# Pools that begin at multiples of 128 bytes, and feed-forward matmuls whose moving operand is read from its last column to its first

## The chip, the cores and the metric

The kernel runs on one core of one Trainium2 chip. The metric is device time in microseconds of one execution: the median of 3 runs before the change is 2208.15 us (2207.96 to 2208.68). Less is better. TensorE (PE in the profile) does the matmuls; PEld is its weight load; VectorE is DVE, ScalarE is ACT, GpSimd is POOL, and SP issues DMAs.

## The reference, cut to what matters

One layer of an encoder over 1024 tokens of width 1024, all in float32: a half-weighted SwiGLU feed-forward, a mixer of two attention branches, and a second feed-forward.

```python
def swiglu(h, w1, w3, w2):
    return (jax.nn.silu(h @ w1) * (h @ w3)) @ w2
...
    h = modulate(x, norm_g[l, 0], mod[:, 0, 0], mod[:, 0, 1])
    x = x + 0.5 * mod[:, 0, 2][:, None, :] * swiglu(h, ffn1_w1[l], ffn1_w3[l], ffn1_w2[l])
    h = modulate(x, norm_g[l, 1], mod[:, 1, 0], mod[:, 1, 1])
    y = hybrid_mixer(h, w_in[l], fox_f_bias[l], ...)
    x = x + mod[:, 1, 2][:, None, :] * y
    h = modulate(x, norm_g[l, 2], mod[:, 2, 0], mod[:, 2, 1])
    x = x + 0.5 * mod[:, 2, 2][:, None, :] * swiglu(h, ffn2_w1[l], ffn2_w3[l], ffn2_w2[l])
```

The hidden width of a feed-forward is 2816. The mixer projects `h`, runs attention over 8 heads with a decay (fox) and over 8 heads with the 256 best keys of an index score (dsa), gates both and projects back.

## The kernel before, in words

Activations lie transposed: 128 features on the partitions, tokens along the free dimension, in halves of 512 tokens. A float32 product is made of three fp32r matmuls (`mm3`, line 465): every operand is split into a high and a low part, and high times high, high times low and low times high are added up in one PSUM bank. So a matmul has a *stationary* operand (128 columns of weights, loaded by a LDWEIGHTS of its own) and a *moving* operand (512 columns that stream through the array).

**The feed-forwards.** Each is done by Strassen's scheme with 7 block products in place of 8. The first half (`UpPair`, line 1496; called up below) runs over 11 pairs of 128 hidden features. A pair has 14 products (7 for each of the two weight matrices), a product runs over 4 blocks of 128 input features, and each block is one `mm3`: 11 x 14 x 4 x 3 = 1848 matmuls with 512 moving columns. Their moving operands are the blocks of `h` in `k.B`: `b11`, `b21`, `b22`, `t1` to `t4`. The gated result is stored in HBM (`d_g`). The second half (`Down`, line 1660) has 7 products over 11 blocks and 4 outputs: 7 x 11 x 4 x 3 = 924 matmuls, again with 512 moving columns, which are blocks of `d_g` read back and split. Up and down of both feed-forwards are 3696 and 1848 matmuls, 5544 together.

**Where operands lie.** SBUF is handed out by pools that begin where the one before them ends. The pool of constants, which is the first on the left, ends 64 bytes past a multiple of 128 in the built program. Tiles are multiples of 128 bytes nearly everywhere, so a pool's tiles all have its remainder. On the right side the pools grow down from an end that is 96 bytes past a multiple of 128. In the built program:

| moving operand of | home | bytes past a multiple of 128 | its weights | matmuls |
|---|---|---|---|---|
| up 1: `b11`, `b21` | `h0`, right | 96 | 96 | 528 |
| up 1: the other five | `h1`, `common0`, left | 64 | 96 | 1320 |
| up 2: `b11`, `b21`, `t2`, `t3` | `h0b`, `h1`, left | 64 | 96 | 1056 |
| up 2: `t1`, `t4`, `b22` | `common`, right | 32 | 96 | 792 |
| down 1 and 2 | same pool as the weights | 96 | 96 | 1848 |

The 528 matmuls of the branches' first part and of the output projection that take `h` tiles have 64 against 96 too.

**The order of the work** is made by a planner (`Plan`, line 213). Every call is recorded as a task with the tiles that it reads and writes; `flush` places the tasks engine by engine by modelled costs, and the program is written in that order. What a task depends on is found from `View.region` (line 136): the part of a tile that a view touches. It looks at the *first* indexing of a view alone; a second indexing of the same view does not narrow the region. Waits on the chip come from the real addresses, not from these regions.

**The attention.** `att_scores` (line 1150) makes the scores of a pair of heads. `mn` is a small tile of 8 columns: the row minima of up to four score tiles go into columns 0 to 3 (by a DVE reduction that also adds the bias, a `CUSTOM_DVE_ANT_0` in the profile and an `ISA pr,mn` in the program), and the sums of the exponentials into columns 4 to 7 (by ACT).

Of the kernel before, what the change touches and what calls it, by code (L numbers as in the profile page):

```python
# [9 lines left out]
F32 = mybir.dt.float32  # L10
# [87 lines left out]
class View:  # L98
# [37 lines left out]
    def region(self):  # L136

        if not self.ops or self.ops[0][0] != "__getitem__":
            return ()
        i = self.ops[0][1][0]  # L140
        r = []
        for j, n in zip(i if isinstance(i, tuple) else (i,), self.tile.full):
            if isinstance(j, slice):
                a, b, step = j.indices(n)
                r.append((a, b))
            elif isinstance(j, int):
                r.append((j, j + 1))
            else:
                break
        return tuple(r)  # L150
# [314 lines left out]
def mm3(k, out, w_hi, w_lo, m_hi, m_lo, start, stop, onto=False):  # L465

    mm = k.nc.tensor.matmul
    kw = dict(skip_group_check=True) if onto else {}
    mm(out, w_hi, m_hi, start=start and not onto, stop=False, **kw)
    mm(out, w_hi, m_lo, start=False, stop=False, **kw)  # L470
    mm(out, w_lo, m_hi, start=False, stop=stop, **kw)
# [82 lines left out]
class Ring:  # L554
# [7 lines left out]
    def raw(self):  # L562
        p, n = self.raws[self.j % len(self.raws)]
        self.j += 1
        return p.tile([128, D], F32, tag="wr", name="wr", bufs=n)
# [23 lines left out]
def t512(k, dt=F32, name="t", home="c"):  # L589

    p, tag, n = k.homes[home]
    return p.tile([128, H], dt, tag=tag, name=name, bufs=n)


class Halves:
# [13 lines left out]
    def raw(self, src, i, home="c", name="wr"):  # L609

        t = t512(self.k, name=name, home=home)
        self.k.nc.sync.dma_start(t, src[:, i * H:i * H + H])
        return t


def part8(w, c):
# [34 lines left out]
def chunks(w):  # L651

    return (1, w) if w <= 512 else (2, w // 2)
# [7 lines left out]
def pview(t, w):  # L661
    n, m = chunks(w)
    return t[:, :w].rearrange("p (a b) -> p a b", a=n)
# [486 lines left out]
def att_scores(k, p, two, j, ps2):  # L1150

    nc = k.nc
    pr = [[], []]
    mn = p.tile([128, 8], F32, tag="mn", name="mn", bufs=6)
    for qbs in ([(2 * j, 2 * j + 1)] if j < 2 else [(2 * j,), (2 * j + 1,)]):
        ps = [ps2() for _ in range(2)]
        nc.want(*ps)
        at = {}
        nc.group = 1 - nc.group
        for qb in qbs:  # L1160
            n, m = chunks((qb + 1) * 128)
            at[qb] = [(qb % 2 if j < 2 else i) * 512 for i in range(n)]
            for i, o in enumerate(at[qb]):
                last = two.diag and i == n - 1
                for t, (a, b) in enumerate(((0, 0), (1, 0), (0, 1))):
                    for h in range(2):
                        r = slice(64 * h, 64 * h + 64)
                        nc.tensor.matmul(ps[h][:, o:o + m], two.q[a][r, qb * 128:qb * 128 + 128],
                                         two.kk[b][r, i * m:i * m + m], start=t == 0, stop=t == 2 and not last)
        for qb in qbs if two.diag else ():  # L1170
            o = at[qb][-1] + chunks((qb + 1) * 128)[1]
            for h in range(2):
                nc.tensor.matmul(ps[h][:, o - 128:o], k.ident_b, k.causal_b, start=False, stop=True)
        nc.group = -nc.group
        yield
        for qb in qbs:
            w = (qb + 1) * 128
            n, m = chunks(w)
            for h in range(2):
                c = 2 * (qb % 2) + h  # L1180
                t = p.tile([128, T], F32, tag="pr", name="pr", bufs=8)
                s = ps[h].rearrange("p (a b) -> p a b", a=2)[:, at[qb][0] // 512:at[qb][0] // 512 + n, :m]
                nc.vector.tensor_tensor_reduce(pview(t, w), s, pview(two.addend(h, qb), w), op0=ALU.add, op1=ALU.min,
                                               scale=1.0, scalar=3e38, accum_out=mn[:, c:c + 1])
                nc.scalar.activation(t[:, :w], t[:, :w], AF.Exp, scale=-1.0, bias=mn[:, c:c + 1],
                                     accum_out=mn[:, 4 + c:5 + c])
                pr[h].append(t)
            yield
    nc.vector.reciprocal(mn[:, 4:8], mn[:, 4:8])
    for h in range(2):  # L1190
        for i, t in enumerate(pr[h]):
            w, c = (2 * j + i + 1) * 128, 4 + 2 * i + h
            nc.gpsimd.tensor_scalar(t[:, :w], t[:, :w], mn[:, c:c + 1], 1.0, op0=ALU.mult, op1=ALU.mult)
        yield
    two.pr = pr
# [219 lines left out]
PAIRS = NF // 2  # L1415


class Operands:
# [26 lines left out]
    def block(self, c):  # L1445

        self.scale(c, 0)
        self.pair("b11" if c < 4 else "b21", self.x[c][0], self.shift(c), "h0")
# [47 lines left out]
class UpPair:  # L1496
# [36 lines left out]

    def block(self, ps, w, b, c, onto=False):
        s = slice(c * 128, c * 128 + 128)
        mm3(self.k, ps, w[0][:, s], w[1][:, s], *self.k.B[b][c], c == 0, c == 3, onto)

    def product(self, src, b, onto=None, bank=None):

# [120 lines left out]
class Down:  # L1660
# [85 lines left out]
    def run(self, steps={}):  # L1746

        k = self.k
        for p, (first, _, early) in enumerate(self.ORDER):
            if p != 1:  # L1750
                ps = [(k.seeded if p in (2, 4, 6) else self.bank)() for _ in range(4)]
            if p == 2:
                for d in range(4):
                    k.nc.scalar.activation(ps[d], self.u[d], AF.Copy)
            ops = []

            def mms(d, q):
                w, m = ops[q]
                c = slice(d * 128, d * 128 + 128)
                mm3(k, ps[d], w[0][:, c], w[1][:, c], *m, q == 0, q == PAIRS - 1, p in (1, 2))  # L1760

            together = PAIRS - 3 if p == 6 else PAIRS
            for q in range(PAIRS):
                for f in steps.get((p, q), ()):
                    f()
                self.step += 1
                self.stores()
                self.loads(p * PAIRS + q + 1 + self.LEAD)
                if early == "s2":
                    self.sum("s2", q)  # L1770
                w = self.wq.split(self.a[first][q])
                ops.append((w, self.wq.split(self.g.pop((p, q)))))
                if early not in (None, "s2"):
                    self.sum(early, q)
                if q < together:
                    for d in range(4):
                        mms(d, q)
            for d in range(4):
                for q in range(together, PAIRS):
                    mms(d, q)  # L1780
                self.out(p, d, ps[d])
                if p == 6 and self.s == 2:
                    self.stores(True)
# [175 lines left out]
def layer(tc, xT, c, pos, ada_w, ada_b, ng, inv, w13a, w2a, w_a, w_f, w_q, w_g, fb, fg, dg, wbr, wout, w13b, w2b, out):  # L1959
    with ExitStack() as es:  # L1960
        k = K()
        k.nc = nc = Plan(tc)

        def pool(stack, name, own=False, **kw):
            if kw.get("space") != DRAM:
                kw["reuse_waits"] = "tile"
            return LatePool(nc, stack.enter_context(tc.tile_pool(name=name, bufs=1, **kw)), kw.get("space"), own)

        k.c = pool(es, "const")
        hp = [None, pool(es, "h1", True)]  # L1970
        k.h_tile = lambda hf, dt=F32R: hp[hf].tile([128, H], dt, tag="h", name="h", bufs=16)
        dp = pool(es, "dram", space=DRAM)
# [48 lines left out]
        with ExitStack() as ph:  # L2021
            k.wq = wq = Halves(k, pool(w0s, "w0", True, side="right"), 8, [nc.vector, nc.gpsimd])
            rp = k.c
# [197 lines left out]
            ps = [k.seeded() for _ in range(4)]  # L2221
# [18 lines left out]
        sp = pool(s3, "s")  # L2240
        k.s = {qb: sp.tile([128, (qb + 1) * 128], F32, name=f"s{qb}") for qb in range(2, 8)}
        k.mask = {qb: sp.tile([128, (qb + 1) * 128], BF16, name=f"mk{qb}") for qb in range(2)}
        for qb in range(2):
            nc.gpsimd.memset(k.mask[qb], 0.0)
            nc.gpsimd.memset(k.mask[qb][0:64, qb * 128 + 64:qb * 128 + 128], BIG)
        k.thr = sp.tile([128, 6], F32, name="thr")
        fox = ExitStack()
        fp = pool(fox, "fox", True, side="right")
        nc.on, nc.window = True, 600
# [22 lines left out]
        ps = ExitStack()  # L2272
# [19 lines left out]
        with ExitStack() as ph:  # L2292
# [9 lines left out]
            for i in range(2):  # L2302
                a, b = (ap.tile([128, H], F32R, tag=f"pz{j}", name=f"pz{j}", bufs=2) for j in "hl")
# [28 lines left out]
        with ExitStack() as ph:  # L2332
            hp[0] = pool(ph, "h0b", True)
            k.wq = wq = Halves(k, pool(ph, "w3", True, side="right"), 8, [nc.vector])
            rp = pool(ph, "rms", True, side="right")
            k.homes = {"h0": (hp[0], "h", 16), "h1": (hp[1], "h", 16), "g": (Pairs(nc, w2, (("wr", 2), ("wh", 2), ("wl", 2))), "g", 12),
                       "c": (pool(ph, "common", True, side="right"), "t", 41)}
            m = br.rest(lambda: next(both))
# [120 lines left out]
```

## Time and profile before

| what | before |
|---|---|
| median of 3 runs | 2208.15 us |
| the profiled execution's span | 2205.4 us |
| its PE busy | 2159.9 us (98%) |
| its DVE busy | 1639.2 us (74%) |
| its ACT busy | 1133.7 us (51%) |
| its POOL busy | 222.1 us (10%) |

The profile tells one execution. Its page gives each engine's busy time; the chain of waits follows back from the last instruction what released what, and merges neighbouring matmuls of one tile name into a row (start in us, length in us, what, count), so a row's length over its count is the time from one matmul's start to the next one's. A table by windows gives each engine's busy time in a stretch. Matmuls overlap in their pipeline, so a matmul's own duration (about 390 ns for 512 columns) is longer than its distance to the next.

By time: the first feed-forward is at 0 to 690 us (down from 466), projections and index scores at 690 to 1025, attention at 1025 to 1380, branches and output at 1380 to 1490, the second feed-forward's up at 1490 to 1991 and its down to the end.

### The profile page before, as it was taken

To read this page: it belongs to the slowest core of one execution; us is meant where nothing else is said; L and a number is where in the kernel's file an instruction comes from. 1 tells how busy PE (TensorE), PEld (TensorE's weight loads), DVE (VectorE), ACT (ScalarE), POOL (GpSimd) and SP (SyncE) were. 2 spreads that over 40 slices of the span, in tenths; PEclk is the share of its full clock that TensorE was granted. 3 is DMA by queue.
4 is the path that set the end of the run, shared out by engine and by line. 5 is a ranking of instruction groups with operands and counts; after the bars stand their busy time and mean duration, and the time that the engine had idled before them with its cause. 6 is when DMAs were issued, how large, how long until landed. Compare 5 with 4: busy or idle time off the path is not lost.

```text
span 2205.4 us, 31519 instructions
## 1 busy us (share of the span) xinstructions
PE 2159.9 (98%) x10700; PEld 1777.8 (81%) x10700; DVE 1639.2 (74%) x3095; ACT 1133.7 (51%) x2101; POOL 222.1 (10%) x229
## 2 busy tenths in 40 slices
PE   7999999999999999999999999999999999999999
PEld 5877888877888999987787777778778888888887
DVE  7977887689876498886896677598865756558665
ACT  4744444445455476776766677234443333334443
POOL 0000212100010201001343233000000000000000
PEclk9999999999999999999999999999999999999999
DMA  9245887699521325456343313696123542367521
GB/s 331 101 134 183 265 281 253 237 360 335 158 88 52 116 91 187 143 162 227 104 155 113 113 48 96 235 340 187 46 76 134 163 124 87 106 215 276 170 74 39
DMA packets 208734, 364.15 MB, mean 165 GB/s; under 512 B 29734, under 2 KB 57382, under 8 KB 208572
## 3 DMA queue, kind: packets, MB, share of 16 engines
q1 hardware_dynamic: 208572, 362.13, 49.1%
q8 instruction: 84, 1.38, 0.3%
q14 instruction: 78, 0.64, 0.1%
HBM read 265.85 MB, written 96.20 MB: 164 GB/s over the span
## 4 chain that ended last, share of the span: by engine, by line
PE 86%; DVE 6%; ACT 3%; DMA 2%; issue 2%; SPq 0%; POOL 0%; DVEq 0%; ACTq 0%; POOLq 0%
PE bs L433 34%; PE b L433 28%; PE pj L433 7%; PE py L433 7%; PE p L433 7%; PE pt L433 3%; DVE xc L433 1%; DVE macc L433 1%; ACT pr L433 1%; DVE wl L433 1%; ACT pth L433 1%; DVE xb L433 1%; DVE ptl L433 0%; SPq L433 0%; DMA gw<-in_w_f 0%
## 5 line engine op out<-in xcount | busy, mean ns | idle before, releaser
L433 PE MATMUL bs<-h,wh 128*128 128x512 f32 x1728 | 542.0, 395 | 1.4 <-ACT bs L433 1.3
L433 ACT ACTIVATE wh<-wr 128x512 fp32r<-128x512 f32 (+1 forms) x330 | 207.3, 638 | 359.0 <-PE bs L433 166.9
L433 PEld LDWEIGHTS bs<-h,wh 128*128 128x128 f32 x1728 | 323.2, 188 | 80.8 <-ACT bs L433 4.8
L433 PE MATMUL b<-h,wh 128*128 128x512 f32 x1088 | 345.2, 397 | 5.2 <-ACT z L433 2.6
L433 PE MATMUL bs<-h,wl 128*128 128x512 f32 x864 | 338.8, 394 | 1.0 <-DVE wl L433 1.0
L433 DVE TENSOR_TENSOR wl<-wr,wh 128x512 fp32r<-128x512 f32 x308 | 209.8, 704 | 127.1 <-ACT wh L433 120.6
L433 PEld LDWEIGHTS b<-h,wh 128*128 128x128 f32 x1088 | 204.9, 189 | 56.1 <-ACT z L433 3.5
L433 PE MATMUL b<-h,wl 128*128 128x512 f32 x544 | 214.9, 395 | 0.7 <-DVE wl L433 0.7
L433 PEld LDWEIGHTS bs<-h,wl 128*128 128x128 f32 x864 | 162.2, 188 | 40.2 <-DVE wl L433 1.9
L433 ACT ACTIVATE wh<-a 128x512 fp32r<-128x512 f32 x132 | 83.3, 631 | 168.6 <-PE b L433 97.5
L433 DVE TENSOR_TENSOR wl<-a,wh 128x512 fp32r<-128x512 f32 x132 | 91.5, 693 | 84.5 <-ACT wh L433 80.6
L433 PE MATMUL b<-wh 128*128 128x512 f32 x352 | 137.2, 390 | 0.7 <-ACT mrow L433 0.7
L433 PE MATMUL b<-wl,wh 128*128 128x512 f32 x352 | 137.0, 389 | 0.0
L433 PE MATMUL b<-wh,wl 128*128 128x512 f32 x352 | 137.0, 389 | 0.0
L433 PEld LDWEIGHTS b<-h,wl 128*128 128x128 f32 x544 | 103.0, 189 | 25.6 <-DVE wl L433 1.6
L433 POOL TENSOR_SCALAR pr<-pr,mn 128x128 f32<-128x128 f32 (+7 forms) x128 | 100.3, 803 | 162.3 <-DVE mn L433 122.5
L433 DVE TENSOR_TENSOR z<-bs,z 128x512 f32<-128x512 f32 x116 | 79.4, 687 | 48.2 <-PE bs L433 27.7
L433 DVE TENSOR_TENSOR wl<-g,wh 128x512 fp32r<-128x512 f32 x154 | 107.0, 695 | 4.2 <-ACT wh L433 4.2
L433 PE MATMUL bs<-wl,wh 128*128 128x512 f32 x264 | 102.8, 391 | 2.1 <-DVE wl L433 1.9
L433 ACT ACTIVATE pr<-pr,mn 128x256 f32<-128x256 f32 (+7 forms) x128 | 98.3, 770 | 11.9 <-DVE mn L433 11.6
L433 DVE SCALAR_TENSOR_TENSOR macc<-mraw,cond,macc 128x512 f32<-128x512 f32 x119 | 96.5, 811 | 10.4 <-DMA mraw<-in_ada_w 8.6
L433 PE MATMUL pj<-wh,h 128*128 128x384 f32 x384 | 102.8, 338 | 0.0
(324 smaller groups left out, 4430.9 us busy)
## 6 DMA issues: line engine op xcount, KB each, us to landing
d_g<-z SPq DMA_DIRECT2D x154, 256.0 KB, 2.0
g<-d_g SPq DMA_DIRECT2D x154, 256.0 KB, 4.4
mraw<-in_ada_w SPq DMA_DIRECT2D x144, 256.0 KB, 5.3
wr<-in_w13a SPq DMA_DIRECT2D x112, 256.0 KB, 5.1
wr<-in_w13b SPq DMA_DIRECT2D x88, 256.0 KB, 4.9
a<-in_w2a SPq DMA_DIRECT2D x44, 256.0 KB, 5.3
a<-in_w2b SPq DMA_DIRECT2D x44, 256.0 KB, 5.4
gw<-in_w_g SPq DMA_DIRECT2D x32, 256.0 KB, 5.2
```

The source lines that it names most:

```text
L433: getattr(getattr(self.tc.nc, e), t.op)(*map(real, t.a), **{n: real(v) for n, v in t.kw.items()})
```

## The change

It has two parts and a helper.

1. Padding. A tile of 64 bytes in front of the constants, one of 96 bytes at the right end of SBUF (a pool of its own, `edge`), one of 96 bytes behind `thr` and one of 64 bytes in the pool `rms`. The tile `mn` is made 32 columns wide, of which the first 8 are used. In the built program every moving and stationary tile of the table above then begins at a multiple of 128 bytes.
2. Direction. `back(t)` is the view `t[:, ::-1]`. All 5544 feed-forward matmuls read their moving operand through it. An up product therefore comes out with its 512 tokens in reverse, is stored so, and down reads it in reverse again, which restores the order. Weights are read as before.
3. `View.region` gives the right bounds for a step of minus one.

```diff
-                r.append((a, b))
+                r.append((a, b) if step > 0 else (b + 1, a + 1))
...
+def back(t):
+
+    return t[:, ::-1]
...
-    mn = p.tile([128, 8], F32, tag="mn", name="mn", bufs=6)
+    mn = p.tile([128, 32], F32, tag="mn", name="mn", bufs=6)[:, 0:8]
...
-        mm3(self.k, ps, w[0][:, s], w[1][:, s], *self.k.B[b][c], c == 0, c == 3, onto)
+        mm3(self.k, ps, w[0][:, s], w[1][:, s], *map(back, self.k.B[b][c]), c == 0, c == 3, onto)
...
-                mm3(k, ps[d], w[0][:, c], w[1][:, c], *m, q == 0, q == PAIRS - 1, p in (1, 2))
+                mm3(k, ps[d], w[0][:, c], w[1][:, c], *map(back, m), q == 0, q == PAIRS - 1, p in (1, 2))
...
         k.c = pool(es, "const")
+        k.c.tile([128, 16], F32, name="pad0")
+        pool(es, "edge", side="right").tile([128, 24], F32, name="pad1")
...
         k.thr = sp.tile([128, 6], F32, name="thr")
+        sp.tile([128, 24], F32, name="pad2")
...
             rp = pool(ph, "rms", True, side="right")
+            rp.p.tile([128, 16], F32, name="pad3")
```

Up to the start of attention every engine's instructions stand in the same order as before; tiles' numbers differ. In attention they move, because of `mn`: it is now a view whose first indexing is `[:, 0:8]`, so its columns all have the same region, and the planner takes every write to one of its columns to wait for each earlier use of any other. On DVE, at the first score blocks of attention (`p_10515` holds the scores of the first head, `p_10517` of the second), stood before:

```order
L433 ISA pr,mn<-p_10515,f 128x128
L433 ISA mn 128x1
L433 ISA pr,mn<-p_10515,f 128x256
L433 ISA mn 128x1
L433 TENSOR_SCALAR tke,tkn<-s_7159,thr 128x384
L433 ISA pr,mn<-p_10517,f 128x128
L433 ISA mn 128x1
L433 ISA pr,mn<-p_10517,f 128x256
```

and now, with `p_10521` the first head's scores and `p_10523` the second's:

```order
L433 ISA pr,mn<-p_10521,f 128x128
L433 ISA mn 128x1
L433 TENSOR_SCALAR tke,tkn<-s_7164,thr 128x384
L433 ISA pr,mn<-p_10523,f 128x128
L433 ISA mn 128x1
L433 TENSOR_SCALAR tkn<-tkn 128x1
L433 TENSOR_SCALAR tke<-s_7164,thr 128x384
L433 ISA pr,mn<-p_10521,f 128x256
```

The reductions of one pair of heads now have other DVE work (the masks' `tke`, `tkn`) between them, and the second block of 256 columns comes after both heads' first. On ACT, at the same place, the exponentials (`pr,mn<-pr,mn`) and the evacuations of other matmuls (`gt`, `qs`, `pzh`, `yt`) stood before:

```order
L433 ACTIVATE pr,mn<-pr,mn 128x128
L433 ACTIVATE pr,mn<-pr,mn 128x256
L433 ACTIVATE pr,mn<-pr,mn 128x128
L433 ACTIVATE pr,mn<-pr,mn 128x256
L433 ACTIVATE gt<-py 128x512
L433 ACTIVATE pzh<-pt 128x384
L433 ACTIVATE pr,mn<-pr,mn 128x384 x2
```

and now:

```order
L433 ACTIVATE pr,mn<-pr,mn 128x128 x2
L433 ACTIVATE gt<-py 128x512
L433 ACTIVATE pr,mn<-pr,mn 128x256
L433 ACTIVATE qs<-pt,g_645 128x512 x2
L433 ACTIVATE pr,mn<-pr,mn 128x256
L433 ACTIVATE pr,mn<-pr,mn 128x384
L433 ACTIVATE pzh<-pt 128x384 x2
```

The exponentials are spread out, with the evacuations between them. From here to the first matmuls of the second feed-forward, orders differ on all engines; behind that they are the same again.

## The prediction

> **What bounds the kernel now.** The page first: how full is each engine, and what is the chain that ended last made of?
>
> ```profile
> span 2205.4 us, 31519 instructions
> PE 2159.9 (98%) x10700; PEld 1777.8 (81%) x10700; DVE 1639.2 (74%) x3095; ACT 1133.7 (51%) x2101; POOL 222.1 (10%) x229
> PEclk9999999999999999999999999999999999999999
> PE 86%; DVE 6%; ACT 3%; DMA 2%; issue 2%; SPq 0%; POOL 0%; DVEq 0%; ACTq 0%; POOLq 0%
> ```
>
> PE is busy nearly throughout, the chain is PE's for 86% of the span, and the clock is granted in every slice. So time is won by making matmuls follow each other faster, and hardly otherwise. Then the table by windows, one for each stage (the two ups, the two downs, attention):
>
> ```profile
> 68.00:466.00 398.00, 395.91 (x1702) 316.91 (x1701) 318.24 (x488) 184.84 (x329) 55.22 (x41) 1.00 0.65 218
> 466.00:690.00 224.00, 221.78 (x985) 181.14 (x984) 184.97 (x303) 118.36 (x208) 11.99 (x9) 1.00 0.57 194
> 1025.00:1380.00 355.00, 342.70 (x2371) 274.40 (x2370) 268.62 (x603) 240.98 (x540) 119.04 (x143) 1.00 0.37 118
> 1490.00:1991.00 501.00, 497.72 (x2153) 401.18 (x2152) 332.74 (x543) 199.43 (x340) 0.00 (x0) 1.00 0.40 129
> 1991.00:2205.40 214.40, 209.74 (x924) 172.97 (x923) 142.53 (x223) 90.55 (x159) 0.00 (x0) 1.00 0.40 132
> ```
>
> The columns are the window, its length, and busy time of PE, PEld, DVE, ACT and POOL, the clock and the DMA share. In the feed-forwards (rows 1, 2, 4, 5) PE lacks 2 to 5 us per stage, and DVE comes next with 318 of 398, 185 of 224, 333 of 501 and 143 of 214 us: 80, 83, 66 and 66%.
>
> Last the chain in order of time, in whose rows neighbouring matmuls are merged. It gives the pace, which is what the change is about:
>
> ```profile
> 68.72 32.33 PE bs L433 x142
> 281.21 11.21 PE bs L433 x48
> 1706.75 10.99 PE bs L433 x48
> 1717.73 11.20 PE b L433 x48
> 1990.97 59.85 PE b L433 x264
> ```
>
> All five rows are matmuls with 512 moving columns at the full clock, and they have four paces. Row 1 is up 1 on `b11`: 32.33 / 142 = 227.7 ns. Row 2 is up 1 on the later operands: 11.21 / 48 = 233.5 ns. Row 3 is up 2 on operands from `common`: 10.99 / 48 = 229.0 ns. Row 4 is up 2 on `h0b` and `h1`: 233.3 ns. Row 5 is down 2: 59.85 / 264 = 226.7 ns. Beside the table of places this sorts itself: with moving operand and weights at the same remainder of 128 bytes (96 and 96) the pace is 226.7 to 227.7 ns; 64 bytes apart it is 229.0; 32 bytes apart, 233.4. So here the place of an operand sets the pace, by up to 6.7 ns a matmul.
>
> **Part 1, the padding.** It makes every relation zero. In the ups 1320 + 1056 = 2376 matmuls go from 233.4 to 226.7 ns, 2376 x 6.7 = 15.9 us; 792 go from 229.0 to 226.7, 1.8 us; 528 and the downs' 1848 have the relation already. Outside the feed-forwards the 528 matmuls of branches and output run at the worst pace too:
>
> ```profile
> 1397.56 2.80 PE bs L433 x12
> ```
>
> 2.80 / 12 = 233.3 ns, so 528 x 6.6 = 3.5 us more. Other projections may gain a little; I count nothing. Sum of the padding: 21.2 us. All of it lies on PE, which sets the end there. The pads themselves are never read or written.
>
> **Part 2, the direction.** The trace has no matmul that reads backwards, so I bound it from both sides. What could a matmul lose at most? A row with 384 columns gives the part that does not grow with them:
>
> ```profile
> 823.05 4.16 PE pj L433 x24
> ```
>
> 4.16 / 24 = 173.3 ns for 384 columns against 226.7 for 512: 0.417 ns a column, so 213.5 ns of a 512-column matmul are streaming and 13.2 ns are fixed. If the direction took all of that away, 5544 x 13.2 = 73 us would go. In the other direction the nearest row is the worst relation, 233.4 ns: if a backward read stood as badly as that everywhere, the feed-forwards would be 528 x 5.7 + 792 x 4.4 + 1848 x 6.7 = 18.9 us slower than before. Farther off stands a matmul at half the clock:
>
> ```profile
> 28.40:31.50 3.10, 3.10 (x8) 2.46 (x8) 3.10 (x6) 2.71 (x6) 0.00 (x0) 0.50 1.05 387
> 28.97 0.63 PE L433 MATMUL b<-h,wl 128*128 128x512 f32 x1
> 29.40 1.05 PE L433 MATMUL b<-h,wh 128*128 128x512 f32 x2
> ```
>
> There one follows the other after 0.43 us at a granted clock of 0.50 (the column before the DMA share). A stream at half the rate would add 5544 x 0.2 = 1109 us.
>
> I take a gain of 6.7 ns, about half the fixed part: the rows show one step of 6.7 ns between the worst and the best relation of two reads, and I take one further step of that size. The reason: the pace hangs on how moving operand and weights lie to each other, so some of the fixed part is their reads' getting in each other's way; and in the built program each weight load is encoded from its last column to its first. Today the two reads run towards each other, afterwards both run downwards from the same remainder. That this helps is an inference; 0 and 13.2 ns stay as ends. 5544 x 6.7 = 37.1 us.
>
> [...]
>
> **Part 3, the moved instructions of attention.** No wait is added on the chip, but DVE's reductions and ACT's exponentials stand in another order.
>
> ```profile
> L433 PE MATMUL p<-qs 64*128 64x512 f32 (+5 forms) x576 | 67.7, 358 | 3.0 <-DVE mn L433 2.7 <-DVE qs L433 0.3
> L433 ACT ACTIVATE pr<-pr,mn 128x256 f32<-128x256 f32 (+7 forms) x128 | 98.3, 770 | 11.9 <-DVE mn L433 11.6
> ```
>
> PE's next scores wait for the reductions to free their bank, today for 2.7 us in all. The cover is PE's other work (projections of the gates, values), queued in order. At worst the second head's reduction of each of 8 pairs and 8 row blocks comes later by one exponential, 64 x 0.77 = 49 us; at best the 355 - 342.7 = 12.3 us that PE idles in attention go. The value is nearest to the small wait: I take +4 us.
>
> **The sum.** 21.2 + 37.1 = 58.3 us off PE. Not all arrives: DVE at 80 to 83% of the first feed-forward goes to some 85% (318 of 398 - 20 us in the up), and waits for DMAs stay as long as they are. I pass on nine tenths, 52.5 us. With attention's 4 us: 48.5 us, so a span of 2156.9 us. The median of the runs is 2.75 us above the profiled span (2208.15 against 2205.4), which makes 2159.7, said as 2160 us.
>
> **The rivals.**
>
> *The direction is indifferent.* Then only the padding is left: 21.2 x 0.9 - 4 = 15 us, 2193 us. For it: the trace has no case of a backward read, and Part 1 stands without it. Against it: reads that disturb each other by their places should also do so by their directions. [...]
>
> *The direction takes the whole fixed part.* 21.2 + 73 = 94 us, of which I pass on 0.85, since DVE in the first feed-forward would then be 87 to 88% busy; less 4 us: 2132 us. [...]
>
> *Slower: the backward read stands badly.* It starts at the last column, 4 bytes below a multiple of 128, and moves against the addresses. If the pace is then that of the worst relation, 233.4 ns everywhere, ups and downs lose 18.9 us, output and branches win 3.5, attention costs 4: 2208.15 + 19.4 = 2228 us. It decides once the feed-forwards' mean passes the present one, (2376 x 233.4 + 792 x 229.0 + 528 x 227.7 + 1848 x 226.7) / 5544 = 230.0 ns. For it: the downs have the best pace already, so 1848 matmuls have that to lose. Against: row 5's pace shows that a relation of zero is good at least forwards. The half-rate read belongs here too, as a far end.
>
> *Nothing happens on PE.* If the paces came from the stages' other work and not from places, only attention's 4 us would remain: 2212 us. Rows 3 and 4 speak against it: they are neighbours in the same stage with the same work, and differ by 4.3 ns.
>
> **How the numbers follow.** Forecast (both parts gain): 0.45. Indifferent: 0.28. Whole fixed part: 0.08. Worst relation or half rate: 0.14. Nothing: 0.05. A measurement of this kernel can tell some 0.2%, 4.4 us, from no change. Faster are the first three, 0.81; within 0.2% is the last, 0.05 (2212 is 0.17% up); slower 0.14. The range reaches from the whole fixed part, 2130, to 2212: it takes in the forecast, the indifferent case, most of the gain's upper end and the case of nothing, and leaves out the slower ones and what lies under 2130, under 0.2. Attention's own ends (-12 to +49 us) are in it only with the forecast and the indifferent case.
>
> **What would show it.** In the chain of the changed kernel 48 up matmuls take 220.0 x 48 = 10.56 us under the forecast, 10.88 if the direction is indifferent, 10.25 if the fixed part goes, 11.2 under the worst relation; a down row of 264 takes 58.1, 59.8, 56.4 or 61.6 us. All up rows should have one pace, whatever the tile: if 11.2 and 10.99 us still stand side by side, the reading of the places is wrong. Output rows of 12 should take 2.72 us. In attention's window PE's idle time should be 12 to 20 us; more means that the moved reductions cost. If the rows show the paces but the span does not follow, DVE or DMAs end the chain in the first feed-forward.

## The result and the profile after

| kernel | median | against before |
|---|---|---|
| before | 2208.06 us (2207.57 to 2208.68) | |
| changed | 2227.57 us (2226.55 to 2230.98) | ratio 1.0097, 95% interval 1.0085 to 1.0108 |

The change makes the kernel 19.5 us slower. The forecast was 2160 us and its range ended at 2212; what happened is the rival "the backward read stands badly", for which the prediction had 2228 us and a chance of 0.14.

The page of the changed kernel first: span, busy time of the engines, and the shares of the chain that ended last.

```profile
span 2229.3 us, 31511 instructions
PE 2173.5 (97%) x10700; PEld 1776.1 (80%) x10700; DVE 1639.2 (74%) x3095; ACT 1133.6 (51%) x2101; POOL 221.4 (10%) x229
PEclk9999999999999999999999999999999999999999
PE 84%; DVE 6%; DMA 4%; ACT 3%; issue 2%; SPq 0%; POOL 0%; DVEq 0%; ACTq 0%; POOLq 0%
```

The same number of matmuls, the same granted clock (mean 0.998 before, 0.997 here), DVE's and ACT's busy time unchanged (1639.2 and 1133.7 us before): PE is still the bound. It lies busy for 13.6 us more and idle for 10.3 us more (2229.3 - 2173.5 = 55.8, before 45.5). So the loss has two sources, one in the matmuls' pace and one in waits. (The profiled execution took 2230.98 us, 3.4 us above the median; so these differences add up to 23.9 us and not to 19.5.) The chain in order of time (start, length, what, count) shows the pace:

```profile
70.68 33.15 PE bs L433 x142
...
273.09 11.20 PE b L433 x48
284.29 11.20 PE bs L433 x48
...
1705.64 11.20 PE bs L433 x48
...
1733.64 11.20 PE b L433 x48
...
2009.04 61.60 PE b L433 x264
```

33.15 / 142, 11.20 / 48 and 61.60 / 264 are all 233.3 to 233.5 ns. The four paces of before have become one, but it is the pace that the worst places had before. The branches' and output's matmuls, which have the padding and read forwards, gained (2.80 us before):

```profile
1413.83 2.72 PE b L433 x12
```

The waits are in attention. The windows cut it from the first score matmul to the first one of the branches; columns are the window, its length, busy time of PE, PEld, DVE, ACT and POOL, clock, DMA share, GB/s. First before, then after:

```profile
1024.50:1381.20 356.70, 344.40 (x2381) 275.87 (x2381) 269.75 (x607) 241.97 (x540) 119.04 (x143) 1.00 0.37 118
```
```profile
1031.90:1405.00 373.10, 350.05 (x2401) 276.77 (x2401) 274.42 (x612) 247.07 (x547) 119.67 (x143) 1.00 0.36 118
```

PE's idle time went from 356.7 - 344.4 = 12.3 us to 23.05 us, past the 12 to 20 us that the prediction had allowed for.

### The profile page after: what moved, and what is told of

It reads as the page before. It is cut to its first block, busy times and chain, and to the rows that moved or that the text cites. A ratio compares the mean times of both kernels' runs of the same rounds, so it can differ in the third digit from the quotient of the medians.

```text
span 2229.3 us, 31511 instructions
## 1 busy us (share of the span) xinstructions
PE 2173.5 (97%) x10700; PEld 1776.1 (80%) x10700; DVE 1639.2 (74%) x3095; ACT 1133.6 (51%) x2101; POOL 221.4 (10%) x229
## 4 chain that ended last, share of the span: by engine, by line
PE 84%; DVE 6%; DMA 4%; ACT 3%; issue 2%; SPq 0%; POOL 0%; DVEq 0%; ACTq 0%; POOLq 0%
PE bs L433 34%; PE b L433 27%; PE pj L433 7%; PE py L433 7%; PE p L433 7%; PE pt L433 2%; DMA mraw<-in_ada_w 1%; DVE macc L433 1%; ACT pth L433 1%; DVE xc L433 1%; DVE wl L433 1%; DMA a<-in_w2a 1%; ACT pr L433 1%; DVE xb L433 1%; SPq L433 0%
## 5 line engine op out<-in xcount | busy, mean ns | idle before, releaser
L433 DVE TENSOR_TENSOR z<-bs,z 128x512 f32<-128x512 f32 x116 | 79.3, 687 | 54.2 <-PE bs L433 31.4
L433 PE MATMUL bs<-wh,wl 128*128 128x512 f32 x264 | 104.3, 397 | 0.0
L433 PE MATMUL bs<-wh 128*128 128x512 f32 x264 | 102.4, 398 | 0.2 <-ACT wh L433 0.2
```

What stands on the lines that cost most here:

```text
L433: getattr(getattr(self.tc.nc, e), t.op)(*map(real, t.a), **{n: real(v) for n, v in t.kw.items()})
```

## The experiments

The theory after the result: the padding gains what was worked out; a backward read costs a matmul 6.7 ns; the moved instructions of attention cost the rest. The rivals: the pads or attention took the time and the direction is innocent; or the direction has good places too, only others than the forward read.

**Taking the three parts apart.** Three kernels, each the changed one with one or two edits undone. `pads_fwd` reads forwards:

```diff
-        mm3(self.k, ps, w[0][:, s], w[1][:, s], *map(back, self.k.B[b][c]), c == 0, c == 3, onto)
+        mm3(self.k, ps, w[0][:, s], w[1][:, s], *self.k.B[b][c], c == 0, c == 3, onto)
...
-                mm3(k, ps[d], w[0][:, c], w[1][:, c], *map(back, m), q == 0, q == PAIRS - 1, p in (1, 2))
+                mm3(k, ps[d], w[0][:, c], w[1][:, c], *m, q == 0, q == PAIRS - 1, p in (1, 2))
```

> The changed kernel with its four pads and its wide mn, but with both feed-forwards reading their moving operand forwards again. Theory (the backward read costs 6.7 ns a matmul, the padding gains as worked out): every feed-forward matmul follows the other after 226.7 to 227.7 ns, 48 up matmuls take 10.88 us and 264 of down 59.85 us; 5544 x 6.7 = 37.1 us off the changed kernel's 2227.6, so about 2190 us. Rival (the direction is innocent, the pads or the moved instructions of attention took the time): rows of 11.2 us stay and the time stays at 2208 us or above.

`after_mn` keeps the backward reads and gives attention its old order; `pads_fwd_mn` has both edits:

```diff
-    mn = p.tile([128, 32], F32, tag="mn", name="mn", bufs=6)[:, 0:8]
+    mn = p.tile([128, 32], F32, tag="mn", name="mn", bufs=6)
```

> As pads_fwd, and mn is indexed directly (32 columns wide, without the view of 8), so that the planner sees its columns apart and attention stands in its old order. Theory: the moved instructions of attention cost some 4 us (what is left of the 19.5 us when the feed-forwards' 18.9 and the 3.5 won in branches and output are taken out), so about 2186 us, 4 below pads_fwd, and PE's idle time in attention returns from 18 to 12 us. Rival (moving them costs nothing on the path): the same as pads_fwd, 2190 us.

> The changed kernel as it is, backward reads and pads, with mn indexed directly, so attention in its old order. Theory: 4 us below the changed kernel, 2223.5 us, all rows of 48 still 11.20 us. Rival (the order of attention costs nothing): 2227.6 us.

| kernel | median | its kernel before | ratio, 95% interval |
|---|---|---|---|
| `pads_fwd` | 2198.3 us | 2208.37 us | 0.9952 (0.994 to 0.9965) |
| `pads_fwd_mn` | 2187.16 us | 2208.37 us | 0.9907 (0.9894 to 0.9921) |
| `after_mn` | 2218.6 us | 2208.37 us | 1.005 (1.0037 to 1.0062) |

Against the kernel before that ran beside them: pads alone -21.2 us, pads and direction +10.2, so the direction costs 31.4 us; all three +19.5, so attention's order costs 9.3 us with backward reads, and with forward ones 2198.3 - 2187.16 = 11.1 us. The chain of `pads_fwd_mn` has the pace that the padding was to give everywhere:

```profile
268.93 10.88 PE b L433 x48
279.81 10.88 PE bs L433 x48
...
1692.52 10.88 PE bs L433 x48
1703.40 10.88 PE b L433 x48
...
1971.11 59.84 PE b L433 x264
```

10.88 / 48 = 59.84 / 264 = 226.7 ns. The first rival falls: pads do no harm. `after_mn` was expected at 2223.5 us; it lies 9.0 us below the changed kernel and not 4, because attention's order costs twice what the theory had left for it. `pads_fwd` was expected at 2190 us; forward reads took 29.3 us off the changed kernel and not 37.1. In `pads_fwd_mn` the two misses cancel, so that its 2187.16 us meet the expected 2186 by luck; it is faster than the kernel before and than the changed one.

**Has the backward read a good place?** `back_unpadded`, the kernel before with the backward read alone, has three relations between the places of moving operand and weights; `back_plus32` has the fourth.

```diff
-        mm3(self.k, ps, w[0][:, s], w[1][:, s], *self.k.B[b][c], c == 0, c == 3, onto)
+        mm3(self.k, ps, w[0][:, s], w[1][:, s], *map(back, self.k.B[b][c]), c == 0, c == 3, onto)
...
-                mm3(k, ps[d], w[0][:, c], w[1][:, c], *m, q == 0, q == PAIRS - 1, p in (1, 2))
+                mm3(k, ps[d], w[0][:, c], w[1][:, c], *map(back, m), q == 0, q == PAIRS - 1, p in (1, 2))
```

> The kernel before with the backward read alone: no pad, mn as before. It has three relations of moving operand and weights: 0, 32 and 64 bytes apart by 128. Theory (a backward read costs its 233.4 ns whatever the relation): all rows of 48 take 11.2 us and rows of 264 61.6 us, 5544 x 3.4 = 18.9 us above the kernel before, about 2227 us. Rival (backward reads have good and bad places too, only others than forward ones, relation zero being their worst): rows of 48 on the left pools (32 bytes apart) or on common (64 apart) fall to 10.9 to 11.0 us while down stays at 61.6; with 226.7 ns at 32 bytes and 229.0 at 64 the mean is 229.9 ns and the time about 2208 us.

Measured 2225.65 us, ratio 1.0082 (1.0066 to 1.0097), so 17.3 us slower. Its chain in the second up:

```profile
1709.97 5.60 PE b L433 x24
1715.57 11.20 PE bs L433 x48
1726.77 11.20 PE b L433 x48
```

The same places with forward reads, in `mn_view` (below), which has every address of the kernel before:

```profile
1711.43 5.51 PE b L433 x24
1716.94 10.99 PE bs L433 x48
1727.93 11.20 PE b L433 x48
```

Forwards the operands from `common` (rows 1 and 2) are faster than those from `h0b` and `h1` (row 3), 229.0 to 229.6 against 233.3 ns; backwards there is no difference, all three rows are at 233.3 ns. `back_plus32` is `after_mn` with one more edit:

```diff
-        k.c.tile([128, 16], F32, name="pad0")
+        k.c.tile([128, 24], F32, name="pad0")
```

> after_mn (backward reads, pads, attention's old order) with the first pad 32 bytes longer, so that the left pools begin 32 bytes past a multiple of 128 and 2376 up matmuls have their moving operand 32 bytes above the weights' remainder, the one relation by 32 bytes that no run has shown backwards; the other 3168 stay at zero. Theory (a backward read has one pace wherever it lies): 233.4 ns for all, after_mn's 2218.6 us plus the 3.5 us that branches and output lose again, 2222 us. Rival (backward reads have a good place that was not met yet): the rows of 48 on the left pools take 10.88 to 11.0 us, 10 to 16 us less, 2206 to 2212 us.

Measured 2224.05 us, ratio 1.0073 (1.0058 to 1.0088), 16.5 us above the kernel before; the rows of 48 in its chain are 11.20 us in both ups. The second rival falls for the four relations by 32 bytes; finer shifts were not tried. Forwards the place counts (226.7 to 234.3 ns) and backwards it doesn't (233.3 to 233.5 ns at all four relations).

**Is it the relation, or the moving operand's own place?** In the feed-forwards of before the weights always lie at 96, so their paces alone can't tell. The projections of the same kernel can: in the built program some of their matmuls with 512 moving columns take the moving operand from `h0` (96 bytes past a multiple of 128) and the weights from the pool `w1` (96) or from the pool `w2` (64). The first row is a stretch of the chain of before with 46 matmuls of the first kind, the second one with 46 of the second:

```profile
943.67 10.45 PE pj L433 x46
```
```profile
858.63 10.78 PE pj L433 x46
```

That is 227.2 ns at the same remainder and 234.3 ns at 32 bytes apart, with the moving operand in the same pool. So forwards it is the relation to the weights that sets the pace. In `pads_fwd_mn` both kinds start at multiples of 128, and matmuls of the second kind take 226.7 ns too:

```profile
852.71 10.43 PE pj L433 x46
```

**The step or the order of the lines?** Five kernels permute the columns in other ways than a full reversal, each a permutation that done twice restores the order. All have the pads and attention's old order; `back` is:

```diff
-    return t[:, ::-1]
+    return t.rearrange("p (a b) -> p a b", a=4)[:, ::-1, :]             # blocks_back
+    return t.rearrange("p (a b) -> p a b", a=4)[:, :, ::-1]             # mid_back
+    return t.rearrange("p (a b) -> p a b", a=16)[:, ::-1, :]            # lines_back
+    return t.rearrange("p (a b) -> p a b", a=16)[:, :, ::-1]            # inner_back
+    return t.rearrange("p (a b c) -> p b a c", a=4, b=4)                # rows_up
```

> Pads and attention's old order as in pads_fwd_mn; the moving operand of the feed-forwards is read as four blocks of 128 columns, the last block first, forwards inside a block (done twice, this restores the order). Theory of the step: what costs is that each column lies before the last one; three of 511 steps go back here, so 226.7 to 227 ns a matmul, 10.88 us for 48, and 2187 us as with forward reads. Theory of the line order: what costs is that the read starts at the upper end and its memory lines come in falling order; then 233.4 ns, 11.20 us for 48 and about 2218.6 us, as with the whole read backwards.

> Pads and attention's old order; four blocks of 128 columns in rising order, backwards inside a block (done twice, this restores the order). The mirror of blocks_back with few jumps. Theory of the step of minus one: 233.4 ns, 11.20 us for 48, about 2218.6 us. Theory of the line order: 226.7 ns, 2187 us. If inner_back's 234.9 ns was its 15 jumps alone, this falls to 227 ns and the step of minus one is innocent.

> As blocks_back with 16 groups of 32 columns (128 bytes), the last group first, forwards inside a group. Theory of the step: 226.7 ns, 10.88 us for 48, 2187 us. Theory of the line order: 233.4 ns, 11.20 us for 48, about 2218.6 us. A cost for each of the 15 jumps would show as a pace above that of blocks_back.

> The reverse of lines_back: 16 groups of 32 columns in rising order, backwards inside each group. Theory of the step: 496 of 511 steps go back, so 233.4 ns, 11.20 us for 48 and about 2218.6 us. Theory of the line order: groups of 128 bytes come in rising order, so 226.7 ns, 10.88 us for 48 and 2187 us.

> Pads and attention's old order; the feed-forwards' moving operand is read forwards inside 16 groups of 32 columns as in lines_back, but the groups come in the order 0, 4, 8, 12, 1, 5 and so on (done twice, this restores the order): 15 jumps as in lines_back, of which 3 fall. If lines_back's 232 ns came from its jumps, this takes 231 to 232 ns a matmul, 11.1 us for 48 and about 2214 us. If they came from falling lines, 3 falls cost as little as in blocks_back: 227 ns, 10.88 us for 48 and 2187 to 2189 us.

The chain's rows, of `blocks_back`, then of `mid_back`:

```profile
266.74 10.88 PE b L433 x48
277.62 10.88 PE bs L433 x48
...
1970.23 59.84 PE b L433 x264
```
```profile
271.38 11.20 PE b L433 x48
282.58 11.20 PE bs L433 x48
...
1996.82 61.60 PE b L433 x264
```

Both have four blocks and three jumps. Starting at the upper end with falling blocks costs nothing (226.7 ns, 2189.3 us, ratio 0.9918, 0.9902 to 0.9935); stepping backwards inside rising blocks costs the whole 6.6 ns (233.3 ns, 2219.16 us, ratio 1.005, 1.0033 to 1.0068). So the step of minus one is what costs, not the falling addresses at large. Down's rows of the three others, `lines_back`, `inner_back` and `rows_up`:

```profile
1991.91 61.34 PE b L433 x264
```
```profile
1999.72 62.48 PE b L433 x264
```
```profile
1996.04 61.60 PE b L433 x264
```

| `back` | jumps, of which fall | step inside | ns, down | median | ratio, 95% interval |
|---|---|---|---|---|---|
| `blocks_back` | 3, 3 | +1 | 226.7 | 2189.3 us | 0.9918 (0.9902 to 0.9935) |
| `mid_back` | 3, 0 | -1 | 233.3 | 2219.16 us | 1.005 (1.0033 to 1.0068) |
| `lines_back` | 15, 15 | +1 | 232.3 | 2214.62 us | 1.0032 (1.0022 to 1.0043) |
| `rows_up` | 15, 3 | +1 | 233.3 | 2220.91 us | 1.0054 (1.0038 to 1.0069) |
| `inner_back` | 15, 0 | -1 | 236.7 | 2224.37 us | 1.0074 (1.0059 to 1.009) |

Neither theory has a price for 15 jumps; the expectation of `lines_back` named one only as a possibility. `lines_back` was expected at 226.7 or 233.4 ns and lies between, and `rows_up`, with mostly rising jumps, is no cheaper than 15 falling ones. So 15 jumps cost 5.6 to 6.6 ns whichever way they go, and three falling ones nothing. Whether it is their number or the shorter runs (32 columns in place of 128) can't be told here, since one follows from the other. The theory of the line order falls (that the memory has lines at all was the author's supposition, which no run shows); that of the step stands for `blocks_back`, `mid_back` and `inner_back`, and needs the jumps beside it. `inner_back` has both costs and they don't add up (11.20 to 11.36 us for 48 in its ups, 233.3 to 236.7 ns, and 236.7 ns in down); why is open.

**A fixed cost, or one by the column?**

```diff
-                mm3(k, ps[tk // m][:, tk % m * n:tk % m * n + n], hh, hl, hi[:, cs], lo[:, cs], i + c == 0,
+                mm3(k, ps[tk // m][:, tk % m * n:tk % m * n + n], hh, hl, back(hi[:, cs]), back(lo[:, cs]), i + c == 0,
```

`proj_n` has the same edit. The kernel doesn't turn the features round again, so that its results are other numbers; it serves for the pace alone.

> pads_fwd_mn with forward feed-forwards, and the projections' moving weights read backwards instead: 768 matmuls with 384 columns, 384 with 256 and 96 with 432. The projected features come out in reverse inside each group, so attention works on other numbers. If the backward read costs a fixed 6.7 ns a matmul: 384 columns 173.3 to 180.0 ns, 256 columns 119.8 to 126.5 ns, in all 1248 x 6.7 = 8.4 us, up to 2195.5 us. If it costs by the column (6.7 / 512 = 0.013 ns): 178.3 and 123.2 ns, 5.7 us, up to 2193 us. If the cost belongs to the 512-column reads alone: no change, 2187 us.

Measured 2188.95 us, ratio 0.9912 (0.9897 to 0.9926), which can't be told from `pads_fwd_mn`. The chain of `pads_fwd_mn`, then of `narrow_back`; the rows of 24 have 384 columns, those of 143 have 256:

```profile
817.25 4.16 PE pj L433 x24
...
915.63 17.16 PE p L433 x143
```
```profile
817.42 4.27 PE pj L433 x24
...
917.28 16.93 PE p L433 x143
```

384 columns: 4.16 / 24 = 173.3 to 177.9 ns, 4.6 more; 256 columns: 120.0 to 118.4 ns, 1.6 *less*. With 6.7 ns at 512 columns none of the three expectations holds. The three fit a cost by the column above a smaller fixed part: (233.3 - 118.4) / 256 = 0.449 ns a column backwards, (226.7 - 120.0) / 256 = 0.417 forwards. The line through both ends gives 175.9 ns at 384, measured 177.9, so it is rough.

**Attention by itself.** The kernel before with one edit that leaves all addresses:

```diff
-    mn = p.tile([128, 8], F32, tag="mn", name="mn", bufs=6)
+    mn = p.tile([128, 8], F32, tag="mn", name="mn", bufs=6)[:, 0:8]
```

> The kernel before with one edit: mn, still 8 columns wide, is handed on as its view of columns 0 to 7, so that every address stays and attention's order is that of the changed kernel. Theory (the moved instructions cost by themselves): pads_fwd less pads_fwd_mn is 11.1 us and the changed kernel less after_mn 9.0 us, so about 2218 us, with PE's idle time in attention up by some 10 us from 12. Rival (the order only hurts together with the pads' places): 2208 us.

Measured 2217.3 us against 2207.73, ratio 1.0047 (1.003 to 1.0063): 9.6 us from the order of instructions alone. Where do they arise? Here are two windows of the same length from the start of attention, the kernel before and `mn_view`:

```profile
1024.50:1396.67 372.17, 358.88 (x2442) 287.25 (x2442) 280.40 (x623) 249.55 (x552) 119.04 (x143) 1.00 0.40 129
```
```profile
1024.65:1396.82 372.17, 350.07 (x2402) 277.10 (x2402) 274.03 (x611) 246.46 (x546) 120.80 (x143) 1.00 0.38 118
```

PE does 40 matmuls less in it and is busy 8.8 us less. What it waits for there (total us, times, longest), before:

```profile
PE py L433 <- DVE ptl L433: 4.4, 11, 1.2
PE p L433 <- DVE mn L433: 2.7, 5, 0.9
PE b L433 <- ACT wh L433: 1.0, 1, 1.0
...
PE py L433 <- ACT pth L433: 0.5, 2, 0.4
```

and in `mn_view`:

```profile
PE py L433 <- ACT pth L433: 7.1, 16, 1.2
PE b L433 <- ACT wh L433: 4.3, 1, 4.3
PE pt L433 <- POOL pr L433: 3.1, 6, 1.2
PE py L433 <- DVE ptl L433: 1.7, 5, 0.3
...
PE p L433 <- DVE mn L433: 0.7, 1, 0.7
```

And on ACT the exponentials (`pr`) and the evacuation of the transposed probabilities (`pth`), before and in `mn_view`; behind the last bar stands ACT's idle time ahead of them, and what ended it:

```profile
L433 ACT ACTIVATE pr<-pr,mn 128x256 f32<-128x256 f32 (+7 forms) x128 | 98.3, 770 | 11.9 <-DVE mn L433 11.6
L433 ACT ACTIVATE pth<-pt 128x512 fp32r<-128x512 f32 x96 | 56.6, 596 | 24.5 <-PE pt L433 22.9
```
```profile
L433 ACT ACTIVATE pr<-pr,mn 128x256 f32<-128x256 f32 (+7 forms) x128 | 99.1, 774 | 22.6 <-DVE mn L433 22.3
L433 ACT ACTIVATE pth<-pt 128x512 fp32r<-128x512 f32 x96 | 54.6, 596 | 14.6 <-PE pt L433 12.8
```

The scores wait less than before. But the exponentials stand in ACT's queue where their minima aren't ready, and ACT stands idle ahead of them for 10.7 us more. Ahead of `pth` it stands idle for 9.9 us less. Read together, this says that `pth` is queued behind the exponentials and finds its input there when ACT comes to it; no run moved one of the two alone. The value products (`py`) on PE wait for `pth`, 7.1 us in place of 0.5. That is the largest term, not the whole: 3.1 us are transposes (`pt`) that wait for probabilities from POOL, and one wait for weights (`wh`) at the start of the branches is 3.3 us longer, while the waits for `ptl` and `mn` are 4.7 us shorter.

## Why the prediction was wrong

**The step that failed** is in Part 2: "I take a gain of 6.7 ns, about half the fixed part", with the reason that weights and moving operand would then be read the same way. The prediction called it an inference, and no row of the trace bore on its sign. Measured, the term is +6.7 ns a matmul against aligned forward reads. 5544 x 6.7 = 37.1 us, of which 31.4 reached the time; the forecast had minus the same 37.1. The reason behind it is contradicted in its outcome: with both operands encoded to be read downwards from the same remainder a matmul takes 233.3 to 233.5 ns, not less than 226.7. Nor does the backward pace depend on the relation of the two places, as the forward one does: it is 233.3 ns at all four. `mid_back` against `blocks_back` (233.3 against 226.7 ns) shows what costs instead: the step of minus one inside a run of columns. Why that step is dearer, no run shows; a disturbance by the weights' read that is the same at every relation isn't ruled out. Reading the weights the other way round, which would have tested the reason at its root, was not tried.

**Part 1 held**, mechanism and size: 21.2 us worked out, 21.2 measured in `pads_fwd_mn`, with a pace of 226.7 ns in its feed-forward rows, and the projections of before bear out that the relation of the two places sets the forward pace (227.2 against 234.3 ns). That the sizes agree to the tenth is luck: PE's busy time fell by 22.8 us (2159.9 to 2137.1), some 1.5 us of it (192 x 7.6 ns) in the projection matmuls that take `h0` and weights from `w2`, which the prediction had left uncounted, and PE's idle time grew by 2.9 us.

**Part 3 was mis-sized, and its cover misjudged**: 4 us were taken, 9.3 to 11.1 measured. The prediction looked at the wait in which DVE's reductions showed up (scores on their bank, 2.7 us), and that one fell to 0.7. The price came through ACT, by what is queued behind the exponentials: in `mn_view` ACT stands idle ahead of them for 10.7 us more, and `py` waits for `pth` for 7.1 us in place of 0.5. The bounds of -12.3 to +49 us held it. The prediction's remark that these bounds stay in the range in the indifferent case is wrong at the upper end: 2193 - 4 + 49 = 2238 us lies above 2212.

**Passing on.** Nine tenths were assumed. Of the padding 21.2 us came against 21.2 counted, of the direction 31.4 / 37.1 = 0.85 on the padded kernel and 17.3 / 18.9 = 0.92 on the unpadded one. In the profiles of `pads_fwd_mn` and `after_mn` PE's busy time differs by 35.2 us (2137.1 and 2172.3) and its idle time by 4.9 us the other way (48.4 and 43.5): part of the slower pace fills waits that were there anyway.

**The rival that came true** had its pace (233.4 ns) and its point of decision right: the feed-forwards' rows are at 233.3 to 233.5, above 230.0. Of its two reasons the start just below a multiple of 128 plays no part, since the pace is the same at all four relations; the movement against the addresses does, as a step of minus one. That its 2228 us meet the measured 2227.57 so closely is partly luck: attention cost some 5 us more than it had, and its 18.9 us of pace arrived by less than the whole. What was wrong was its chance. For the direction the trace bounded the size on both sides and said nothing about the sign; 0.53 on a gain and 0.14 on a loss rested on the inference alone.

## What to carry to other kernels

For fp32r matmuls with 512 moving columns and a weight load each, as here, begin the pools of TensorE's operands at one remainder of 128 bytes, here worth 1% (2187.16 against 2208.37 us), and let the moving operand run forwards in long runs: a step of minus one, or 15 jumps in 512 columns, gave all of that back and more (2214.62 to 2224.37 us). With 256 columns the step was no loss (118.4 against 120.0 ns). A term for which the trace has no row of either sign deserves about even chances on both sides, however neat the mechanism. And a change of one small tile's indexing can reorder a planned program: look for what is queued behind the instructions that moved, on each engine (here ACT's `pth` behind the exponentials), not only at the waits in which they show up today.

## What the runs showed of the hardware that was not expected

- 512-column fp32r matmuls with the moving operand read at step -1: 233.3 to 233.5 ns, at each of the four relations of places by 32 bytes; forwards 226.7 ns at relation zero, 229.0 at 64 bytes apart, 233.3 to 234.3 at 32. Forwards it is the relation to the weights that counts, not the moving operand's own place: 227.2 against 234.3 ns with the same `h0` and other weights.
- The cost grows with the columns and turns: +6.7 ns at 512, +4.6 at 384, -1.6 at 256.
- Three falling jumps among 512 columns are free (226.7 ns); fifteen cost 5.6 to 6.6 ns, whether all fall or most rise.
